# Attention with a score bias on one Trainium2 core: rearranging the first ten microseconds of a kernel bound by ScalarE

## The chip, the cores and the metric

The kernel runs on one core of a Trainium2 chip. The metric is the device time of one execution in microseconds (us); lower is better. The *span* is the stretch from the first to the last instruction in the profile of an execution; it was 1.7 to 3.0 us shorter than the time. Engines: PE (TensorE matmul; PEld is its weight load), DVE (VectorE), ACT (ScalarE), POOL (GpSimd), SP (SyncE).

## The reference

Shapes are 4 x 8 x 1024 x 64 for q, k and v, and 1 x 1 x 1024 x 1024 for the bias, all float32.

```python
scores = scale * np.matmul(q, k.transpose(0, 1, 3, 2)) + bias
scores_max = np.max(scores, axis=-1, keepdims=True)
attn = np.exp(scores - scores_max) / (np.sum(np.exp(scores - scores_max), axis=-1, keepdims=True) + 1e-8)
return np.matmul(attn, v).astype(np.float32)
```

## The kernel before

The kernel uses exp(s + b) = exp(s) * exp(b). PE makes scores in PSUM, "slots" of up to three banks of 128 x 512; ACT takes exp of a slot (tile `E`); DVE multiplies it by exp(bias) (tile `eb`); PE multiplies the result with V, in which a column of ones gives the row sum. exp(bias) is made once, in four pieces: PE transposes the bias (tile `pb`), ACT takes its exp. All loads but the first four go through one software DMA queue issued by POOL, in the order below.

```python
nc.sync.dma_start(out=k0f[:, :, :2]..., in_=kf[0]...)      # first k quarter, float32
nc.scalar.dma_start(out=q0f[0]..., in_=qf[0]...)           # q, head 0, first half
nc.sync.dma_start(out=q0f[1]..., in_=qf[0]...)             # q, head 1, first half
nc.sync.dma_start(out=k0f[:, :, 2:]..., in_=kf[0]...)      # second k quarter
# ... POOL: k half, q half, first bias half, k and q of pair 1
wm = ps_s.tile([P, 3, HQ], F32, tag="s", name="wm")
for i in range(6):                                         # dummy matmuls: keep PE busy
    nc.tensor.matmul(wm[:, i % 3, :], zeros[:, :P], zeros[:], start=True, stop=True)
# ...
nc.vector.tensor_copy(qr0[:, 0, :QC, :], q0f[0][:])        # casts to bf16
nc.scalar.copy(kr0[:, :, :2, :], k0f[:, :, :2, :])
nc.scalar.copy(qr0[:, 1, :QC, :], q0f[1][:])
pq0 = q_trans(0, ...); pk0 = k_trans(0, 2, "xb"); q_out(0, pq0)
nc.scalar.copy(kr0[:, :, 2:QC, :], k0f[:, :, 2:, :])       # the late k cast
nc.scalar.copy(kT0[:, :2, :], pk0[:])                      # the first k copy
pq1 = q_trans(1, ...)
s_fill(0); q_out(1, pq1); s_exp(0)
pk1 = k_trans(2, 2, "xa")
s_fill(1); nc.vector.tensor_copy(kT0[:, 2:QC, :], pk1[:]); s_exp(1)
# from here on a small scheduler in Python orders the rest; order is ACT's order:
order = [("S", g) for g in range(2, NS)]
for at, x in ((5, (0, 0)), (7, (0, 4)), (11, (1, 0)), (13, (1, 4))):
    order.insert(at, ("B",) + x)                           # the four bias exps
# ... behind the second k half's copy:
nc.vector.memset(vall[:, :, :, D:D1], 1.0)                 # ones
load_v(0); nc.gpsimd.dma_start(out=btraw[:, QC:, :], ...)  # V of pair 0, second bias half
load_v(1); load_qk(2)
```

The scheduler's result is a fixed order of instructions on each engine; each engine carries it out in that order.

The softmax here doesn't subtract the row's maximum and nothing guards it: scores larger than these inputs give would overflow.

Of the kernel before, what the change touches and what calls it, by code (L numbers as in the profile page):

```python
# [15 lines left out]
def kernel(  # L16
# [15 lines left out]
    nc = tc.nc  # L32
    B, H, S, D = q.shape
    P = 128
    NCH = S // P
    D1 = D + 1
    NP = B * H // 2
    scale = 1.0 / (D ** 0.5)
    HQ = S // 2
    QC = NCH // 2  # L40
# [5 lines left out]
    bf_ = bias.rearrange("a b (p c) k -> p (a b c) k", p=P)  # L46
# [12 lines left out]
    btraw = consts.tile([P, NCH, S], BF)  # L59
# [3 lines left out]
    vall = consts.tile([P, 2 * NP, NCH, D1], BF)  # L63

    k0f = consts.tile([P, 2, QC, D], F32)
    q0f = [consts.tile([P, QC, D], F32, name=f"q0f{t}") for t in range(2)]
    zeros = consts.tile([P, HQ], BF)
# [4 lines left out]
    def load_qk(pr):  # L72
        qr = raw.tile([P, 2, NCH, D], BF, name="qr")
        kr = raw.tile([P, 2, NCH, D], BF, name="kr")
        nc.gpsimd.dma_start(out=kr.rearrange("p t c d -> p t (c d)"), in_=kf[pr])  # L75
        nc.gpsimd.dma_start(out=qr.rearrange("p t c d -> p t (c d)"), in_=qf[pr])  # L76
        raws[pr] = (qr, kr)

    def load_v(pr):
        for t in range(2):  # L80
            nc.gpsimd.dma_start(out=vall[:, 2 * pr + t, :, :D], in_=vf[pr, :, t])  # L81
# [30 lines left out]
    NS = len(slots)  # L112
# [3 lines left out]
    def e_at(b, n):  # L116
        if b // ET not in etiles:
            etiles[b // ET] = ep.tile([P, ET, HQ], BF, name="E")
        return etiles[b // ET][:, b % ET:b % ET + n, :]
# [3 lines left out]
    def s_fill(g):  # L123
        ps = ps_s.tile([P, 3, HQ], F32, tag="s", name="ps")
        open_ps[("S", g)] = ps
        for j, b in enumerate(slots[g]):
            pr, h, qh, kc = banks[b]
            qT, kT = trs[(pr, 0)], trs[(pr, 1)]
            nc.tensor.matmul(ps[:, j, :], kT[:, kc, :], qT[:, h, qh * HQ:(qh + 1) * HQ],  # L129
                             start=True, stop=b not in late_bias)  # L130
            if b in late_bias:
                nc.tensor.matmul(ps[:, j, :], ident[:], braw[:, late_bias[b], :], start=False, stop=True)

    def s_exp(g):
        n = len(slots[g])
        nc.scalar.activation(e_at(slots[g][0], n), open_ps.pop(("S", g))[:, :n, :], ACTF.Exp, scale=scale)  # L136
# [26 lines left out]
    def late_bias_pe(tag):  # L163

        px = ps_x.tile([P, 2, HQ], BF, tag=tag, name="px")
        for j in range(2):
            for i in range(QC):
                nc.tensor.transpose(px[:, j, i * P:(i + 1) * P],
                                    btraw[:, QC + i, :].rearrange("p (kp kc) -> p kc kp", kc=NCH)[:, NCH - 2 + j, :],
                                    ident[:])  # L170

        def copy():
            nc.vector.tensor_scalar(braw[:], px[:], 1.0 / scale, None, op0=ALU.mult)
        return copy
# [39 lines left out]
    with tc.manual_schedule():  # L214
# [9 lines left out]
        qr0 = raw.tile([P, 2, NCH, D], BF, name="qr")  # L224
        kr0 = raw.tile([P, 2, NCH, D], BF, name="kr")
        raws[0] = (qr0, kr0)
        kT0 = kvp.tile([P, NCH, P], BF, name="kT")
# [11 lines left out]
        load_qk(1)  # L239

        wm = ps_s.tile([P, 3, HQ], F32, tag="s", name="wm")
        for i in range(6):
            nc.tensor.matmul(wm[:, i % 3, :], zeros[:, :P], zeros[:], start=True, stop=True)

        def k_trans(c0, n, tag):
            px = ps_x.tile([P, n, P], BF, tag=tag, name="px")
            for c in range(n):
                for t in range(2):
                    nc.tensor.transpose(px[t * D:(t + 1) * D, c, :], kr0[:, t, c0 + c, :], ident[:])
            return px  # L250

        def q_trans(t, px):
            for c in range(QC):
                nc.tensor.transpose(px[t * D:(t + 1) * D, c, :], qr0[:, t, c, :], ident[:])
            return px

        def q_out(t, px):
            nc.vector.tensor_copy(qT0[t * D:(t + 1) * D, t, :HQ],
                                  px[t * D:(t + 1) * D, :, :].rearrange("p c q -> p (c q)"))

        nc.vector.tensor_copy(qr0[:, 0, :QC, :], q0f[0][:])
        nc.scalar.copy(kr0[:, :, :2, :], k0f[:, :, :2, :])
        nc.scalar.copy(qr0[:, 1, :QC, :], q0f[1][:])
        pq0 = q_trans(0, ps_x.tile([P, QC, P], BF, tag="xa", name="px"))
        pk0 = k_trans(0, 2, "xb")
        q_out(0, pq0)
        nc.scalar.copy(kr0[:, :, 2:QC, :], k0f[:, :, 2:, :])
        nc.scalar.copy(kT0[:, :2, :], pk0[:])
        pq1 = q_trans(1, ps_s.tile([P, 3, 2 * HQ], BF, tag="s", name="pq").rearrange(
            "p b (c q) -> p (b c) q", q=P)[:, :QC, :])  # L270
        s_fill(0)
        q_out(1, pq1)
        s_exp(0)
        pk1 = k_trans(2, 2, "xa")
        s_fill(1)
        nc.vector.tensor_copy(kT0[:, 2:QC, :], pk1[:])
        s_exp(1)



        COLD = 4600
        EXP, EXP0, QK, AV, TP = 427, 45, 216, 170, 350
        MUL, COPYQ, COPYK, EVAC, SEM = 600, 650, 420, 620, 80
        order = [("S", g) for g in range(2, NS)]
        for at, x in ((5, (0, 0)), (7, (0, 4)), (11, (1, 0)), (13, (1, 4))):
            order.insert(at, ("B",) + x)
        NO = len(order)
        T0 = 5250.0
        t_act, t_pe, t_dve = T0 + 1620, T0 + 550, T0 + 600
        filled = []  # L290
        act_end = []
        x_free = {"xa": T0 + 600, "xb": T0}
        x_unit = {}
        bias_at = [13000, 22000]
        raw_at = {0: (5900, 6600), 1: (15500, 16500), 2: (26000, 28500)}
        pieces = [(0, 1, 1), (0, 0, 1)]
        for pr in range(1, NP):
            pieces += [(pr, 1, 0), (pr, 0, 0), (pr, 1, 1), (pr, 0, 1)]

        pieces.append((NP, 0, 0))  # L300
        raw_at[NP] = (T0, T0)
        piece_end = {(0, 1, 0): T0 + 600, (0, 0, 0): T0}
        eb_at = {}
        exp_at = {0: T0 + 600, 1: T0 + 1620, 2: T0 + 1620}
        mul_at = {}
        mul_next = 0
        av_order = []
# [7 lines left out]
        def unit_of(b):  # L315
            return banks[b][:3]
# [10 lines left out]
        def act_end_of(i):  # L327
            if i < 0:
                return T0
            if i < len(act_end):  # L330
# [30 lines left out]
        def pe_piece():  # L361
            if not pieces:
                return None
            pr, which, half = pieces[0]
            if pr not in raw_at or (pr < NP and pr not in raws):
                return None
            i = min(len(filled), NO - 1)
            while order[i][0] != "S":
                i -= 1
            at = slots[order[i][1]][0]  # L370
            if at < (pr - 2) * 32 + 8:
                return None

            left = NCH - av_next % NCH
            busy = x_unit.get(unit_of(av_order[av_next])) if av_next % NCH else None
            tags = sorted((x_free[x], x) for x in x_free if x != busy)
            if busy and left < 4 and at < pr * 32 - 16:
                return None
            if not busy and av_next and at < pr * 32 - 16 and tags[0][0] + SEM < t_pe and len(tags) > 1 and tags[1][0] > t_pe:
                return None  # L380
            free, tag = tags[0]
            ready = max(free + SEM, raw_at[pr][1 - which])

            def emit(t):
                pieces.pop(0)
                copy = transpose_pe(pr, which, half, tag) if pr < NP else late_bias_pe(tag)
                cost = COPYK if which else COPYQ
                x_free[tag] = 1e12

                def run(t2):  # L390
                    copy()
                    if (pr, which, half) == (0, 1, 1):
                        nc.vector.memset(vall[:, :, :, D:D1], 1.0)  # L393
                        load_v(0)
                        nc.gpsimd.dma_start(out=btraw[:, QC:, :], in_=bf_[:, QC:, :])
                        load_v(1)
                        load_qk(2)
                    x_free[tag] = t2 + cost
                    piece_end[(pr, which, half)] = t2 + cost
                    if pr < NP and which == 0 and half == 1:  # L400
                        if pr + 3 < NP:
                            load_qk(pr + 3)
                            raw_at[pr + 3] = (t2 + 7000, t2 + 7000)
                        if pr + 2 < NP:
                            load_v(pr + 2)
                dve_q.append((t + pe_cost(t, TP) + SEM, 0, cost, run))
            return ready, TP, emit
# [84 lines left out]
        while len(act_end) < NO or av_next < NB or dve_q:  # L492
# [12 lines left out]
            if who == 0:  # L505
                i = a[2]
                item = order[i]
                t_act = t + a[1]
# [11 lines left out]
            elif who == 1:  # L520
                if d in dve_q:
                    dve_q.remove(d)
                t_dve = t + d[2]
                d[3](t)
            else:
                t_pe = t + pe_cost(t, p[1])
# [31 lines left out]
```

## Time and profile before

| | before |
|---|---|
| time, median of the first three executions | 251.33 us (251.31 to 251.9) |
| span of the profiled execution | 250.1 us |
| ACT busy | 239.9 us (96%) |
| exp 3 (the exp of slot 3) starts | 10.92 us |
| second bias half lands | 24.2 us |
| third bias exp starts | 25.56 us, after 0.24 us of idle |

The lines are shown in the prediction. In a timeline line the first number is the start in us, the second the time from the first start to the last end of the merged instructions, then engine, source line, operation and tiles; brackets hold the idle time of the engine before it and what ended it.

### The profile page before, as it was taken

The page shows a single profiled execution, that of the slowest core. Times are in us where ns is not written, and L with a number is a line of the kernel's source. Part 1 is how long each engine was busy: PE and PEld are TensorE (multiplying, and loading weights), DVE is VectorE, ACT ScalarE, POOL GpSimd, SP SyncE. Part 2 cuts the span into 40 slices and gives each one's busy share as a digit, 9 for nine tenths or more (in the row PEclk, how much of TensorE's full clock was granted, in tenths as well). Part 3 has the DMA queues.
Part 4 walks back from the last instruction along what each step waited for, and adds up shares of the span by engine and source line. Part 5 has one row for each costly group of instructions (what it writes and reads, how often), then busy time and mean ns, then how long its engine had stood idle before and what let it go on. Part 6 is the DMA issues. An engine that isn't in the chain of part 4 may idle for free.

```text
span 250.1 us, 7172 instructions
## 1 busy us (share of the span) xinstructions
PE 231.5 (93%) x3152; PEld 141.8 (57%) x3152; DVE 219.1 (88%) x375; ACT 239.9 (96%) x182; POOL 53.7 (21%) x74
## 2 busy tenths in 40 slices
PE   6868999999999999999999999999999999999893
PEld 2345756556566556665566656666665555665552
DVE  4209699999999999999999999999999999998884
ACT  4799999999999999999999999999999999999991
POOL 8183505161040131302213055016000000000000
PEclk9999999999999999999999999999999999999999
DMA  6999997799186393920935859728911102020112
GB/s 119 189 187 181 192 144 122 55 155 180 45 134 79 82 89 99 114 87 8 167 62 103 91 74 184 83 84 105 111 44 42 46 0 88 3 84 3 62 46 64
DMA packets 48175, 23.79 MB, mean 95 GB/s; under 512 B 34448, under 2 KB 44048, under 8 KB 47888
## 3 DMA queue, kind: packets, MB, share of 16 engines
q0 software_dynamic: 42272, 14.42, 53.4%
q1 hardware_dynamic: 5584, 8.72, 9.6%
q8 instruction: 24, 0.39, 0.6%
q10 hardware_dynamic: 288, 0.20, 0.3%
q14 instruction: 7, 0.06, 0.1%
HBM read 29.36 MB, written 8.39 MB: 151 GB/s over the span
## 4 chain that ended last, share of the span: by engine, by line
ACT 75%; PE 16%; DVE 5%; DMA 1%; issue 1%; SPq 0%; DVEq 0%; ACTq 0%
ACT E L136 73%; PE ps L129 11%; PE px L89 2%; ACT eb L149 2%; PE po L186 2%; DVE E L161 2%; DMA k0f<-in_k_dram 1%; DVE E L158 1%; PE pb L144 1%; DVE qT L98 1%; DVE E L155 1%; DVE oall L206 0%; DVE rs L196 0%; SPq L218 0%; SPq L216 0%
## 5 line engine op out<-in xcount | busy, mean ns | idle before, releaser
L136 ACT ACTIVATE E<-ps 128x1536 bf16<-128x1536 f32 (+2 forms) x172 | 230.2, 1709 | 2.2 <-PE ps L129 2.2
L129 PE MATMUL ps<-qT,kT 128*128 128x512 bf16 x512 | 139.5, 381 | 10.0 <-ACT E L136 5.4
L186 PEld LDWEIGHTS <-E 128*128 128x128 bf16 x2048 | 83.1, 98 | 38.8 <-DVE E L158 2.1
L158 DVE TENSOR_TENSOR E<-E,eb 128x2048 bf16<-128x2048 bf16 x82 | 98.9, 1217 | 1.3 <-ACT E L136 0.7
L186 PE MATMUL po<-vall,E 128*128 128x65 bf16 x2048 | 92.9, 194 | 1.8 <-DVE E L158 0.8
L129 PEld LDWEIGHTS <-kT 128*128 128x128 bf16 x512 | 45.5, 97 | 44.7 <-issue 9.4
L161 DVE TENSOR_TENSOR E<-E,eb 128x1024 bf16<-128x1024 bf16 x84 | 55.8, 684 | 7.7 <-ACT eb L149 6.8
L81 POOL DMA_DIRECT2D vall<-in_v_dram x32 | 28.2, 885 | 10.0 <-DVE vall L393 5.5
L75 POOL DMA_DIRECT2D kr<-in_k_dram x15 | 10.6, 704 | 91.8 <-PE px L89 91.5
L206 DVE TENSOR_TENSOR oall<-po,rs 128x256 f32<-128x256 f32 x63 | 26.7, 425 | 2.2
L98 DVE TENSOR_TENSOR qT<-px,mask 128x1024 bf16<-128x1024 bf16 x31 | 21.5, 694 | 3.3 <-PE px L89 2.0
L102 DVE COPY kT<-px 128x512 bf16<-128x512 bf16 x31 | 13.1, 422 | 4.9 <-PE px L89 4.4
L76 POOL DMA_DIRECT2D qr<-in_q_dram x15 | 10.8, 720 | 18.5 <-PE px L89 16.8
L196 DVE RECIPROCAL rs<-po 128x4 f32<-128x4 f32 x64 | 11.4, 178 | 3.8 <-PE po L186 3.3
L89 PE MATMUL px<-ident,kr 128*64 128x128 bf16 x248 | 13.0, 227 | 0.2 <-DVE oall L206 0.2
L89 PE MATMUL px<-ident,qr 128*64 128x128 bf16 x248 | 13.1, 228 | 0.0
L89 PEld LDWEIGHTS <-qr 128*64 128x64 bf16 x248 | 8.1, 111 | 7.9 <-issue 6.4
L89 PEld LDWEIGHTS <-kr 128*64 128x64 bf16 x248 | 8.1, 110 | 7.1 <-issue 5.4
L149 ACT ACTIVATE eb<-pb 128x2048 bf16<-128x2048 bf16 x4 | 7.5, 1877 | 0.2 <-PE pb L144 0.2
L144 PE MATMUL pb<-ident,btraw 128*128 128x128 bf16 x64 | 4.6, 225 | 1.5 <-ACT eb L149 1.0
L144 PEld LDWEIGHTS <-btraw 128*128 128x128 bf16 x64 | 4.5, 147 | 1.9 <-issue 1.7
L155 DVE TENSOR_TENSOR E<-E,eb 128x1024 bf16<-128x1024 bf16 (+1 forms) x6 | 4.6, 776 | 0.6 <-ACT E L136 0.6
(39 smaller groups left out, 22.0 us busy)
## 6 DMA issues: line engine op xcount, KB each, us to landing
out_dram<-oall SPq DMA_DIRECT2D x30, 256.0 KB, 2.1
vall<-in_v_dram POOLq DMA_DIRECT2D x32, 128.0 KB, 6.5
kr<-in_k_dram POOLq DMA_DIRECT2D x15, 256.0 KB, 4.2
qr<-in_q_dram POOLq DMA_DIRECT2D x15, 256.0 KB, 5.7
btraw<-in_bias_dram POOLq DMA_DIRECT2D x2, 1024.0 KB, 10.0
out_dram<-oall SPq DMA_DIRECT2D x3, 128.0 KB, 1.7
k0f<-in_k_dram SPq DMA_DIRECT2D x2, 128.0 KB, 3.0
q0f<-in_q_dram ACTq DMA_DIRECT2D x1, 128.0 KB, 2.6
```

The costliest lines, as they stand in the source:

```text
L81: nc.gpsimd.dma_start(out=vall[:, 2 * pr + t, :, :D], in_=vf[pr, :, t])
L89: nc.tensor.transpose(px[t * D:(t + 1) * D, c, :], src[:, t, half * QC + c, :], ident[:])
L98: nc.vector.tensor_tensor(dst[:, :, half * HQ:(half + 1) * HQ], px.rearrange("p c q -> p (c q)").unsqueeze(1).to_broadcast([P, 2, HQ]), ma ...
L102: nc.vector.tensor_copy(dst[:, half * QC:(half + 1) * QC, :], px[:])
L129: nc.tensor.matmul(ps[:, j, :], kT[:, kc, :], qT[:, h, qh * HQ:(qh + 1) * HQ], start=True, stop=b not in late_bias)
L136: nc.scalar.activation(e_at(slots[g][0], n), open_ps.pop(("S", g))[:, :n, :], ACTF.Exp, scale=scale)
L144: nc.tensor.transpose(ps[:, j, i * P:(i + 1) * P], btraw[:, qh * QC + i, :].rearrange("p (kp kc) -> p kc kp", kc=NCH)[:, k0 + j, :], ident[:])
L149: nc.scalar.activation(eb[:, qh, k0:k0 + 4, :], open_ps.pop(("B", qh, k0))[:, :4, :], ACTF.Exp)
L158: nc.vector.tensor_tensor(e, e, eb[:, qh, kc:kc + 2, :].unsqueeze(2).to_broadcast([P, 2, 2, HQ]), op=ALU.mult)
L161: nc.vector.tensor_tensor(e, e, eb[:, qh, kc:kc + 1, :].to_broadcast([P, n, HQ]), op=ALU.mult)
L186: nc.tensor.matmul(acc[:, i, :], e[:, 0, i * P:(i + 1) * P], vall[:, 2 * pr + h, kc, :], start=(kc == 0 and i == 0), stop=(kc == NCH - 1), ...
L206: nc.vector.tensor_tensor(oall[:, c0:c0 + QC, :], acc[:, :, :D], rs[:].to_broadcast([P, QC, D]), op=ALU.mult)
```

## The change

The intent is an earlier and gapless start of ACT's stream of exps. The second q cast leaves ACT for DVE, the late k cast goes behind the copy that frees the first score matmul, and the second k half is transposed before slot 2, so that slot 3 does not wait for it. The ones, and with them the V loads, come sooner. The dummy matmuls are trimmed to end before the first data come.

```diff
-        for i in range(6):
-            nc.tensor.matmul(wm[:, i % 3, :], zeros[:, :P], zeros[:], start=True, stop=True)
+        def dummy(n):
+            nc.tensor.matmul(wm[:, 0, :n], zeros[:, :P], zeros[:, :n], start=True, stop=True)
+        for i in range(5):
+            dummy(HQ)
+        dummy(P)
 ...
-        nc.scalar.copy(qr0[:, 1, :QC, :], q0f[1][:])
+        nc.vector.tensor_copy(qr0[:, 1, :QC, :], q0f[1][:])
 ...
-        nc.scalar.copy(kr0[:, :, 2:QC, :], k0f[:, :, 2:, :])
         nc.scalar.copy(kT0[:, :2, :], pk0[:])
         pq1 = q_trans(1, ...)
-        s_fill(0)
         q_out(1, pq1)
+        nc.scalar.copy(kr0[:, :, 2:QC, :], k0f[:, :, 2:, :])
+        dummy(P)
+        s_fill(0)
         s_exp(0)
         pk1 = k_trans(2, 2, "xa")
         s_fill(1)
         nc.vector.tensor_copy(kT0[:, 2:QC, :], pk1[:])
+        nc.vector.memset(vall[:, :, :, D:D1], 1.0)
         s_exp(1)
+        pk2 = k_trans(QC, QC, "xb")
+        s_fill(2)
+        nc.vector.tensor_copy(kT0[:, QC:, :], pk2[:])
+        s_exp(2)
+        load_v(0)
+        nc.gpsimd.dma_start(out=btraw[:, QC:, :], in_=bf_[:, QC:, :])
+        load_v(1)
+        load_qk(2)
 ... (the scheduler's starting times are set to match; the issues leave their old place)
```

ACT's order is unchanged from slot 3 on. On PE the second q half's transposes, which stood ahead of slot 3, now stand behind slot 4.

More of the change, by code (lines that the diff above doesn't have):

```diff
@@ L270 @@
             "p b (c q) -> p (b c) q", q=P)[:, :QC, :])
+        q_out(1, pq1)
+        nc.scalar.copy(kr0[:, :, 2:QC, :], k0f[:, :, 2:, :])
+        dummy(P)
         s_fill(0)
-        q_out(1, pq1)
         s_exp(0)
@@ L283 @@
         MUL, COPYQ, COPYK, EVAC, SEM = 600, 650, 420, 620, 80
-        order = [("S", g) for g in range(2, NS)]
-        for at, x in ((5, (0, 0)), (7, (0, 4)), (11, (1, 0)), (13, (1, 4))):
+        order = [("S", g) for g in range(3, NS)]
+        for at, x in ((4, (0, 0)), (6, (0, 4)), (10, (1, 0)), (12, (1, 4))):
             order.insert(at, ("B",) + x)
         NO = len(order)
-        T0 = 5250.0
-        t_act, t_pe, t_dve = T0 + 1620, T0 + 550, T0 + 600
+        T0 = 7000.0
+        t_act, t_pe, t_dve = T0 + 1400, T0, T0 + 300
         filled = []
         act_end = []
-        x_free = {"xa": T0 + 600, "xb": T0}
+        x_free = {"xa": T0 - 500, "xb": T0 + 200}
         x_unit = {}
-        bias_at = [13000, 22000]
-        raw_at = {0: (5900, 6600), 1: (15500, 16500), 2: (26000, 28500)}
-        pieces = [(0, 1, 1), (0, 0, 1)]
+        bias_at = [13000, 21500]
+        raw_at = {0: (5900, 7000), 1: (15500, 16500), 2: (26000, 28500)}
+        pieces = [(0, 0, 1)]
         for pr in range(1, NP):
@@ L301 @@
         raw_at[NP] = (T0, T0)
-        piece_end = {(0, 1, 0): T0 + 600, (0, 0, 0): T0}
+        piece_end = {(0, 1, 0): T0, (0, 0, 0): T0, (0, 1, 1): T0 + 200}
         eb_at = {}
-        exp_at = {0: T0 + 600, 1: T0 + 1620, 2: T0 + 1620}
+        exp_at = {x: T0 + (0 if x < 3 else 1400) for x in range(6)}
         mul_at = {}
@@ L391, in run @@
                     copy()
-                    if (pr, which, half) == (0, 1, 1):
-                        nc.vector.memset(vall[:, :, :, D:D1], 1.0)
-                        load_v(0)
-                        nc.gpsimd.dma_start(out=btraw[:, QC:, :], in_=bf_[:, QC:, :])
-                        load_v(1)
-                        load_qk(2)
                     x_free[tag] = t2 + cost
```

## The prediction

> **What bounds the kernel now.** I began with the page's busy shares: ScalarE (ACT) is busy 239.9 us of a span of 250.1 us, so it idles 10.2 us in all, and its own work outside the prologue is not touched by the change. VectorE has 219.1 us and PE 231.5 us. The chain of work that ended last says the same:
>
> ```profile
> PE 231.5 (93%) x3152; PEld 141.8 (57%) x3152; DVE 219.1 (88%) x375; ACT 239.9 (96%) x182; POOL 53.7 (21%) x74
> ...
> ACT 75%; PE 16%; DVE 5%; DMA 1%; issue 1%; SPq 0%; DVEq 0%; ACTq 0%
> ```
>
> So the change can only pay through ACT's idle time. The timeline of ACT over the first 30 us (start, duration, what, and in brackets the idle time before it and what ended it) shows where that is:
>
> ```profile
> 3.58 0.41 ACT L262 CAST kr<-k0f 128x256 bf16<-128x256 f32 x1 [0.89 <-DMA k0f<-in_k_dram]
> 3.92 0.41 ACT L263 CAST qr<-q0f 128x256 bf16<-128x256 f32 x1
> 5.00 0.40 ACT L267 CAST kr<-k0f 128x256 bf16<-128x256 f32 x1 [0.68 <-DMA k0f<-in_k_dram]
> 5.31 0.37 ACT L268 COPY kT<-px 128x256 bf16<-128x256 bf16 x1
> 6.37 0.60 ACT L136 ACTIVATE E<-ps 128x512 bf16<-128x512 f32 x1 [0.70 <-PE ps L129]
> 7.69 1.02 ACT L136 ACTIVATE E<-ps 128x1024 bf16<-128x1024 f32 x1 [0.72 <-PE ps L129]
> 8.97 1.45 ACT L136 ACTIVATE E<-ps 128x1536 bf16<-128x1536 f32 x1 [0.26 <-PE ps L129]
> 10.92 5.48 ACT L136 ACTIVATE E<-ps 128x1536 bf16<-128x1536 f32 x4 [0.49 <-PE ps L129]
> ...
> 21.19 4.13 ACT L136 ACTIVATE E<-ps 128x1536 bf16<-128x1536 f32 x3
> 25.56 1.88 ACT L149 ACTIVATE eb<-pb 128x2048 bf16<-128x2048 bf16 x1 [0.24 <-PE pb L144]
> ```
>
> The reader is to see two things. First, ACT has waits of 0.68, 0.70, 0.72, 0.26 and 0.49 us before the fourth exp (I call the exps of the score slots exp 0, 1, 2, 3); from 10.92 us on it runs without a gap, up to the third bias exp (eb) at 25.56 us, which waits 0.24 us for the bias transposes. After that no ACT idle of over 0.1 us follows until the tail. Second, the change works on the first stretch alone, and eb at 25.56 is a second gate behind it. What feeds that gate is in the timeline of PE and POOL at that time:
>
> ```profile
> 24.10 0.42 PE L186 MATMUL po<-vall,E 128*128 128x65 bf16 x8 [0.37 <-DVE E L158]
> 24.33 1.06 PEld L144 LDWEIGHTS <-btraw 128*128 128x128 bf16 x16
> 24.36 1.17 PE L144 MATMUL pb<-ident,btraw 128*128 128x128 bf16 x16
> 24.50 0.88 POOL L81 DMA_DIRECT2D vall<-in_v_dram  x1 [3.80 <-DMA btraw<-in_bias_dram]
> ```
>
> The second half of the bias is issued at 13.19 us (L395), and the tile's view gives 11.0 us as its longest time to landing: 24.2 us. POOL, which waits for that landing too, goes on at 24.50. PE starts the transposes at 24.36, so at most about 0.15 us after the data. In the table by stretch the DMA share stays full all along:
>
> ```profile
> 8.00:12.00 4.00, 3.53 (x25) 1.49 (x24) 1.32 (x3) 3.25 (x3) 0.57 (x1) 1.00 1.03 211
> 12.00:16.00 4.00, 2.51 (x21) 1.51 (x21) 0.00 (x0) 4.00 (x4) 4.00 (x6) 1.00 1.52 174
> 16.00:20.00 4.00, 3.19 (x49) 2.33 (x47) 1.79 (x4) 4.00 (x4) 2.56 (x5) 1.00 1.20 195
> 20.00:24.00 4.00, 3.20 (x33) 1.53 (x31) 3.70 (x6) 4.00 (x4) 0.70 (x1) 1.00 1.50 174
> ```
>
> The last two columns are the DMA share and GB/s: the software queue is never without work from about 4 us to 35 us.
>
> **What the Trainium skill says.** (1) "TensorE: Matmul & The Clock Gate", section "What's actually happening": PE starts at half rate, and a free-running window of about 3.4 us that was busy enough releases it. The trace agrees: the weight loads of the first score matmuls start at 7.02, 7.45 and 7.88 us, 0.43 us apart, while three such matmuls at 12.42 us take 0.81 us together, which is 0.22 us apart. So PE was still slow while it fed exps 1 and 2; the clock column says 1.00 throughout and does not show this. (2) "DMA: Bandwidth & Descriptors", section "Queues, rings and completion order": each engine consumes its ring's descriptors in order (said of the hardware queues). The software queue's landings agree: they come in the order of issue. (3) The same page, "Latency and other measured facts", says that two of the DMA engines are usually slower, with contention from the software descriptor rings as a guess. The trace is compatible: V of pair 0 needed until 18.5 us although the q load ahead of it landed at 15.7, and later V loads land about 1 us apart. (4) "ScalarE: Activation LUTs", "What ACT_TABLE_LOAD costs": back-to-back ACTIVATEs overlap by about 93 ns. Here four exps of 1.45 us take 5.48 us, 1.34 us each, so it agrees.
>
> **The change part by part.** All times below are from the start of the span; "est." is worked out from the rows above.
> - *Dummies.* Six of 0.427 us become five and one of 128 columns (0.107 us): they end 0.32 us sooner, near 3.5 us, so the first q transposes start after VectorE's cast (3.32 + 0.29 = 3.61) at 3.65 est. and not 3.91.
> - *Second q cast to VectorE.* It removes 0.41 us from ACT and adds about 0.29 us to an idle VectorE; its data lands near 3.9 us either way, so its transposes hardly move.
> - *Late k cast behind the first k copy.* Before, the copy stood behind a cast that waited until 5.00 for its DMA, and ran at 5.31. Now it can run when the k transposes end, 4.6 to 4.75 est., and ends near 5.0. The first score matmul goes from 5.73 to about 5.0 to 5.1, and exp 0 from 6.37 to about 5.7. The late cast then runs at 5.0 to 5.4, as before, so the next k transposes come at 5.45 est. in place of 6.27, and exp 1 near 6.9 in place of 7.69.
> - *Second k half ahead of slot 2.* Eight transposes come before the three matmuls of slot 2. Before, slot 2 followed slot 1 at once, and then came 16 transposes, a copy of 0.42 us and the wait for it. Now: transposes from 6.8 (8.87 less the 2.1 us of five matmuls, carried to the new slot 1), slot 2 at about 7.35 and ready at 7.35 + 2 x 0.427 + 0.63 = 8.83 if PE is still slow. Exp 2 then runs 8.85 to 10.2, and slot 3 is ready long before, so exp 3 starts at 10.2 in place of 10.92: 0.7 us gained. If PE comes to full rate near 6.9 (fewer gaps on PE make a busy window likelier), slot 2 is ready at 7.9 and exp 3 starts at about 9.3: 1.6 us gained.
> - *Ones ahead of the V loads.* The memset (0.27 us) moves from 10.85 to about 6.3, so POOL issues V and the second bias half 4 to 5 us sooner. In a queue that is busy all along and kept in order, that by itself brings no byte earlier.
> - *Order behind the prologue.* ACT's order is unchanged from exp 3 on. On PE the third bias transposes now stand ahead of the eight AV matmuls that waited for VectorE at 24.10. That makes them wait for the landing alone.
>
> So ACT reaches the gate 0.7 to 1.6 us sooner. Beside that gate its idle time was 0.24 us. If the bias half lands at 24.2 as before, the transposes run 24.25 to 25.4, eb starts at 25.45, and all that is kept is about 0.1 us; the idle time before eb becomes 0.24 + 0.7 to 1.6 less 0.1. Every microsecond that the landing itself moves forward is kept, up to the head start. So gain = 0.1 + (24.2 - new landing), at most about 1.7.
>
> **The rivals.** *A, the landing does not move* (about 40%): for it, the full DMA share and the ordered queue. Time 251.33 - 0.1 = 251.2. *B, it moves by 0.3 to 1.5 us* (about 50%): the excess of some 1.7 us in V of pair 0 falls in the time in which POOL writes descriptors without a pause (its busy time is 4.00 of 4 us at 12 to 16); with these issues moved to 6.5 to 10 us, that stall may shrink. The author's own table also sets the arrival of the second bias half 0.5 us earlier. Time 251.33 - 0.1 - 0.3 to 1.5: 249.8 to 250.9, its middle 250.4. *C, it gets worse* (about 10%): the first bias half (issued at 3.97, needed by PE at about 13.5 now and not 15.11) is slowed by POOL's earlier descriptor work, or the k half lands too late for its new place. Time 251.4 to 251.9.
>
> **Range and chances.** 0.4 x 251.2 + 0.5 x 250.4 + 0.1 x 251.6 = 250.8. The range is 250.0 to 251.5; it takes in the spread of the kernel before (251.31 to 251.9) on the side of A. Two per cent is 5.0 us, and ACT's whole idle time ahead of eb is less than that if the start-up before 3.58 us is left out, so same has 0.98, and the other two 0.01 each.
>
> **What would show it right or wrong.** In the changed profile: the first score matmul at 5.0 to 5.2; exp 0 near 5.7; exp 1 near 6.9; exp 3 between 9.2 and 10.3; score matmuls 0.43 or 0.22 us apart at 7.3 say which end. Then the idle time before the third eb: about 1 us or more with "PE pb" as the releaser shows A; near zero with bias transposes well before 24 us shows B. I am wrong if exp 3 starts after 10.5 (the prologue chain is not what I think), or if the time falls by more than 1.7 us, or if a new ACT wait turns up at 12 to 24 us.

## The result, and the profile after

The changed kernel takes 251.29 us (median of 6, 250.83 to 251.81), the kernel before 251.25 us (median of 6, 250.47 to 251.9). The ratio is 1.0007 with a 95% interval of 0.9985 to 1.0029: the same. By their record, which calls a difference under 2% the same, every run that has a verdict is the same as the kernel before; what is said below of smaller differences rests on the intervals and on the spans.

The profiled execution has a span of 249.1 us, 1.0 us less than the first profile of before. ACT's timeline in it:

```profile
4.54 0.37 ACT L272 COPY kT<-px 128x256 bf16<-128x256 bf16 x1 [0.53 <-PE px L254]
4.95 0.41 ACT L276 CAST kr<-k0f 128x256 bf16<-128x256 f32 x1
5.65 0.60 ACT L136 ACTIVATE E<-ps 128x512 bf16<-128x512 f32 x1 [0.30 <-PE ps L129]
6.42 7.92 ACT L136 ACTIVATE E<-ps 128x1024 bf16<-128x1024 f32 x6 [0.17 <-PE ps L129]
...
24.54 1.88 ACT L149 ACTIVATE eb<-pb 128x2048 bf16<-128x2048 bf16 x1 [1.21 <-PE pb L144]
```

The exps run from 6.42 us without a gap; exp 3 starts at 8.87 us (taken from the single records of the merged line), 2.05 us sooner than in the first profile of before. But the idle time ahead of the third bias exp has grown from 0.24 to 1.21 us. The timeline of PE and POOL there:

```profile
23.32 1.04 PEld L144 LDWEIGHTS <-btraw 128*128 128x128 bf16 x16 [1.69 <-DMA btraw<-in_bias_dram]
23.33 1.18 PE L144 MATMUL pb<-ident,btraw 128*128 128x128 bf16 x16 [1.57 <-ACT E L136]
23.57 0.88 POOL L81 DMA_DIRECT2D vall<-in_v_dram  x1 [4.48 <-DMA btraw<-in_bias_dram]
```

PE's weight load waited 1.69 us for the bias to land (23.28 us), and ACT waited for PE. That is half of the story. The other half is the durations of the first score matmuls, in the tile view of `ps` (durations in ns as min/median/max, then first and last start). The first profile of before, 4 to 10.2 us:

```profile
L129 PE MATMUL ps<-qT,kT x7: 587/634/634, 5.7 to 9.9; 128*128 128x512 bf16 x7
```

The changed kernel, 4 to 8 us:

```profile
L129 PE MATMUL ps<-qT,kT x9: 376/379/390, 5.2 to 7.9; 128*128 128x512 bf16 x9
```

In the first, PE was at half rate up to slot 3; in the second it was at full rate for all of them. The trace's clock record gives the moment: 10.30 us in the first profile of before, 5.25 us in this one. The experiments ask whether that belongs to the kernel or to the single execution.

### The profile page after: what moved, and what is told of

It is laid out like the page before. It is cut to its first block, busy times and chain, and to the rows that moved or that the text cites. A ratio compares the mean times of both kernels' runs of the same rounds, so it can differ in the third digit from the quotient of the medians.

```text
span 249.1 us, 7119 instructions
## 1 busy us (share of the span) xinstructions
PE 226.9 (91%) x3098; PEld 141.4 (57%) x3153; DVE 219.2 (88%) x376; ACT 239.6 (96%) x181; POOL 53.6 (22%) x74
## 4 chain that ended last, share of the span: by engine, by line
ACT 79%; PE 14%; DVE 4%; issue 1%; DVEq 0%; ACTq 0%
ACT E L136 76%; PE ps L129 8%; ACT eb L149 3%; PE po L186 2%; PE px L89 2%; PE wm L244 1%; DVE E L161 1%; DVE E L158 1%; DVE E L155 1%; DVE qT L98 1%; PE pb L144 0%; PE px L254 0%; DVE kT L102 0%; PE px L259 0%; DVE oall L206 0%
## 5 line engine op out<-in xcount | busy, mean ns | idle before, releaser
L129 PE MATMUL ps<-qT,kT 128*128 128x512 bf16 x457 | 134.6, 377 | 11.9 <-ACT E L136 5.2
L75 POOL DMA_DIRECT2D kr<-in_k_dram x15 | 10.5, 701 | 94.7 <-PE px L89 91.8
L102 DVE COPY kT<-px 128x512 bf16<-128x512 bf16 x30 | 12.6, 421 | 2.4 <-PE px L89 1.9
L76 POOL DMA_DIRECT2D qr<-in_q_dram x15 | 10.8, 717 | 18.3 <-PE px L89 16.8
L89 PE MATMUL px<-ident,kr 128*64 128x128 bf16 x240 | 12.4, 225 | 0.3 <-DVE oall L206 0.3
## 6 DMA issues: line engine op xcount, KB each, us to landing
btraw<-in_bias_dram POOLq DMA_DIRECT2D x2, 1024.0 KB, 11.5
```

What stands on the lines that cost most here:

```text
L89: nc.tensor.transpose(px[t * D:(t + 1) * D, c, :], src[:, t, half * QC + c, :], ident[:])
L102: nc.vector.tensor_copy(dst[:, half * QC:(half + 1) * QC, :], px[:])
L129: nc.tensor.matmul(ps[:, j, :], kT[:, kc, :], qT[:, h, qh * HQ:(qh + 1) * HQ], start=True, stop=b not in late_bias)
```

## The experiments

Theory one, *the gate*: the third bias exp cannot start before the second bias half lands plus about 1.25 us, so a head start ahead of it is lost. Theory two, formed after e5, *the clock*: the head start depends on when PE comes to full rate, which the change makes late more often. "Slow" and "late" mean this half rate at the start. The rival throughout is that the rest of the kernel, or one part of the change, holds the time.

The table collects all 14 profiles. "Full rate" is from the trace's clock record. In that record the clock drops again 238.93 us after its release in nine profiles and 242.35 us after it in five: a difference of 3.41 us, the length of the stretches used here. "Busy share" is PE's busy share in the 3.41 us before that moment and, after the stroke, in the 3.41 us before those (a dash where that stretch starts more than 1 us before PE's first work). I worked it out from the matmuls' starts, a matmul of 512 columns counted as 0.427 us, of 384 as 0.320 and of 128 as 0.107 us (their spacing in the traces while slow), and time in which two overlap counted once. "Waits" are ACT's idle times of 0.1 us or more behind exp 3.

| profile | full rate, us | busy share | exp 3, us | waits, us | span, us |
|---|---|---|---|---|---|
| before | 10.30 | 0.92 / 0.61 | 10.92 | 0.24 | 250.07 |
| e1, before again | 5.58 | 0.78 / - | 9.93 | 0.34 | 249.16 |
| e4 | 9.66 | 0.91 / 0.66 | 10.66 | 0.22 | 249.77 |
| e6 | 9.22 | 0.89 / 0.73 | 10.43 | 0 | 249.22 |
| e11 | 4.06 | 0.74 / - | 9.47 | 0 | 248.24 |
| changed | 5.25 | 0.82 / - | 8.87 | 1.21 | 249.06 |
| e2, changed again | 5.14 | 0.84 / - | 9.46 | 0.53 + 0.26 | 249.27 |
| e3 | 7.80 | 0.74 / 0.71 | 10.08 | 0.33 | 249.31 |
| e5 | 9.44 | 0.85 / 0.64 | 10.96 | 0 | 249.76 |
| e7 | 10.88 | 0.83 / 0.72 | 10.74 | 0 | 249.52 |
| e8 | 10.70 | 0.87 / 0.68 | 10.74 | 0.27 | 249.90 |
| e9 | 5.68 | 0.83 / - | 9.24 | 0.86 | 248.98 |
| e10 | 9.60 | 0.88 / 0.74 | 10.74 | 0 | 249.52 |
| e12 | 10.59 | 0.92 / 0.73 | 10.79 | 0 | 249.61 |

In every row the span less exp 3 less the waits is 238.8 to 239.0 us. So nothing behind exp 3 makes a difference but those waits, and the whole question is exp 3 and the waits. The time less the span differs by up to 1.3 us between executions, so the spans are the finer measure.

### e1 and e2: both kernels once more

No edit. Expected of e1:

> The kernel before, once more, for the spread of its start. First theory (the second bias half is the gate): the third bias exp starts 1.2 to 1.4 us after that half lands, or when the exps ahead of it end, whichever is later, and nothing ahead of it counts. In the first profile of before PE went to full rate near 10.3 us and the half landed at 24.2 us; if both are matters of the single execution, they differ here (landing anywhere from 23.2 to 24.3 us), and the time follows the landing. Rival (the later landing is a property of the kernel before, made by its late V issue): it lands at 24.2 us again, within 0.2 us, with V of pair 0 again landing near 18.5 us.

Expected of e2:

> The changed kernel once more. Gate theory: the bias half lands at 23.2 to 24.2 us and the third bias exp starts 1.2 to 1.3 us later, with about 1.0 to 2.0 us of ACT idle ahead of it, whatever exp 3 did. Rival (the head start is lost elsewhere): no idle time before that exp in this execution, and a wait of 1 us or more at some later place.

Measured: 251.2 us for before, 251.03 us for the changed kernel, one execution each. The timeline of ACT, kernel before (e1):

```profile
9.93 5.48 ACT L136 ACTIVATE E<-ps 128x1536 bf16<-128x1536 f32 x4 [0.73 <-PE ps L129]
...
24.66 1.88 ACT L149 ACTIVATE eb<-pb 128x2048 bf16<-128x2048 bf16 x1 [0.34 <-PE pb L144]
```

and the changed kernel (e2):

```profile
8.11 6.82 ACT L136 ACTIVATE E<-ps 128x1536 bf16<-128x1536 f32 x5 [0.68 <-PE ps L129]
15.47 1.88 ACT L149 ACTIVATE eb<-pb 128x2048 bf16<-128x2048 bf16 x1 [0.53 <-PE pb L144]
...
24.75 1.88 ACT L149 ACTIVATE eb<-pb 128x2048 bf16<-128x2048 bf16 x1 [0.26 <-PE pb L144]
```

The kernel before now had full rate at 5.58 us and its bias half landed at 23.4 us, with V of pair 0 at 17.2 and not 18.5 us. So the 1 us between the two first spans was a matter of the executions, not of the change. The rival of e1 falls. In e2 the bias half landed at 23.5 us and the third bias exp started at 24.75 us, so the gate holds, though not with the 1 to 2 us of idle that I had named: the head start had already gone. The k half landed at 6.9 us (5.85 in the first profile of the changed kernel), too late for its new place ahead of slot 2, so exp 2 waited 0.68 us. The first bias half landed at 14.2 us (13.0 there), so the first bias exp waited 0.53 us. The gate has sisters.

### e3 and e4: the second bias half one place ahead in the queue

```diff
-        load_v(0)
+        load_v(0, (0,))
         nc.gpsimd.dma_start(out=btraw[:, QC:, :], in_=bf_[:, QC:, :])
+        load_v(0, (1,))
         load_v(1)
```

e3 is this in the changed kernel, e4 in the kernel before (`load_v` gets a second argument: which of the two heads).

> The changed kernel with one queue entry moved: the second bias half is issued after the first V load and not after the second, so it should land about 0.95 us sooner (near 22.3 us). Gate theory: ACT's idle time before the third bias exp falls from 1.21 us to about 0.3 us and the time falls by 0.7 to 1.0 us against the kernel before (ratio near 0.9965). Rival (the gain is lost elsewhere, the wait before that exp is only where it shows): the time stays within 0.2 us of the kernel before, and the idle time turns up at a later place.

> The same move of the queue entry in the kernel before, without the change of the prologue. Gate theory: there ACT comes to the third bias exp only 0.24 us too early, so no more than about 0.25 us is won (ratio 0.999 to 1.0), however early the half lands; its prologue becomes the bound. Rival (the order of the loads alone makes the time): it wins as much as the changed kernel does with the same move, 0.7 us or more.

Measured: e3 251.37 us, ratio 1.0008 (0.9981 to 1.0034); e4 251.26 us, ratio 0.9996 (0.9969 to 1.0024). The expectation for e3 failed at its first step: the half landed at 23.5 us in both, no sooner than behind two V loads. The trace's packet records show the last data packet of that half ending at 21.50 us in e3 and 21.47 us in e4, so 2 us passed between data and landing; in the changed kernel it was 22.67 us and 23.28 us. A landing is counted by 16 increments of a semaphore: 15 of them had come by 21.77 us in e3 and 21.79 us in e4, and the last came at 23.52 and 23.55 us. Why is left open. And e3 reached full rate only at 7.80 us, so exp 3 started at 10.08 us. The two results do not tell the theories apart.

### e5 and e6: the third and fourth bias exps one slot later

```diff
-        for at, x in ((4, (0, 0)), (6, (0, 4)), (10, (1, 0)), (12, (1, 4))):
+        for at, x in ((4, (0, 0)), (6, (0, 4)), (11, (1, 0)), (13, (1, 4))):
```

e6 is the same in the kernel before (11 to 12, 13 to 14).

> The changed kernel with the third and fourth bias exps one score slot later in the schedule, so ACT has one more exp of 1.34 us to do before it comes to the gate. In five of six traces so far the span is the start of the third bias exp plus 224.5 us. Gate theory: the idle time ahead of that exp goes (under 0.2 us), the head start shows at last, the span is the start of exp 3 plus 238.9 us (247.8 to 249.0 us for exp 3 at 8.9 to 10.1) and the time falls by 0.7 to 1.5 us against the kernel before (ratio 0.994 to 0.997). Rival (the rest of the kernel is bound by VectorE or AV work, not by ACT's start): the time stays within 0.3 us of before, with new ACT waits behind 30 us, since the multiplications of the second half now start later.

> The same move of the two bias exps in the kernel before. Gate theory: ACT came to the gate only 0.24 to 0.34 us too early there, so 0.2 to 0.4 us is won and no more (ratio near 0.999); exp 3 at about 10 to 11 us is then the bound. Rival (the order of the exps is itself what helps): as much is won as in the changed kernel.

Measured: e5 251.45 us, ratio 1.0007 (0.9979 to 1.0035); e6 250.4 us, ratio 0.9966 (0.993 to 1.0002). e6 won 0.34%, more than the 0.2 to 0.4 us that I expected, but its interval takes in 1. Neither profile has a wait at the gate. That is no test of the gate, though: in e5 the half landed at 22.37 us, and the exp at its old place, 1.34 us earlier at about 25.3 us, would not have waited either (in e6 it would have met the gate just on time). And e5 won nothing. ACT's timeline of e5:

```profile
6.34 0.60 ACT L136 ACTIVATE E<-ps 128x512 bf16<-128x512 f32 x1 [0.52 <-PE ps L129]
7.66 1.02 ACT L136 ACTIVATE E<-ps 128x1024 bf16<-128x1024 f32 x1 [0.72 <-PE ps L129]
9.62 6.82 ACT L136 ACTIVATE E<-ps 128x1536 bf16<-128x1536 f32 x5 [0.93 <-PE ps L129]
...
26.61 1.88 ACT L149 ACTIVATE eb<-pb 128x2048 bf16<-128x2048 bf16 x1
```

and the tile view of `ps` in it, 4 to 9.3 us:

```profile
L129 PE MATMUL ps<-qT,kT x6: 582/619/634, 5.7 to 8.9; 128*128 128x512 bf16 x6
```

PE was slow up to 9.44 us, exp 2 waited 0.93 us for the eight transposes and three slow matmuls now ahead of it, and exp 3 started at 10.96 us, no sooner than in the kernel before. So the gate alone does not explain the result: in this execution there was no head start to lose. Five of the six spans of e5 stand at 249.5 to 249.8 us, one at 248.9. The changed kernel's six are alike: 249.1 once, 249.5 to 249.7 five times. The kernel before spreads wider in the same rounds as e5: 248.5 to 249.1 us seven times and 249.6 to 250.4 four times. That made the second theory. What PE did between the dummies and the first transposes of e5:

```profile
2.49 1.17 PE L244 MATMUL wm<-zeros 128*128 128x512 bf16 x3
4.26 0.53 PE L259 MATMUL px<-ident,qr 128*64 128x128 bf16 x3 [0.60 <-DVE qr L266]
```

The first q load landed at 3.88 us there (3.27 in the first profile of the changed kernel). The trimmed dummies were used up at 3.45 us, and PE had a hole of 0.8 us up to 4.26 us (the bracket says 0.60, since it counts from the end of the last dummy's latency, not of its columns) in the stretch that should have released its clock: busy share 0.64.

A late load was not the whole of it. Where the first q load landed at 3.51 to 3.65 us (e3, e6, e7, e8, e10, e11, e12), VectorE's cast behind it took 0.42 to 0.56 us and not 0.29, and ended at 4.09 to 4.10 us in all seven. DVE's timeline of e7:

```profile
3.53 0.56 DVE L266 CAST qr<-q0f 128x256 bf16<-128x256 f32 x1 [0.64 <-DMA q0f<-in_q_dram]
```

POOL was busy with the issue of the q half from 3.25 to 3.98 us in each of them; whether that held up the cast was not tested.

### e7 and e8: both moves, and the late V loads back

e7 has the edits of e3 and e5 together. e8 is e5 with the ones, V loads and second bias half issued behind the copy of the second q half.

> Both moves in the changed kernel: bias half issued after the first V load, and its exp one slot later. The first move brought the landing no sooner in e3 and e4 (23.5 us), so gate theory: the same as e5 within 0.3 us, without idle time ahead of the third bias exp. Rival (the landing still binds): e7 is faster than e5 by 0.5 us or more.

> e5 with one part of the change undone: ones, V loads and the second bias half issued behind the q half as late as before (near 11 us in place of 7.6 to 8.2 us). If the early issue does nothing, because the queue is full and ordered: landings as in e5 (bias half 23.2 to 24.2 us), time as e5 within 0.3 us. Rival (the late issue costs landing time, as the first trace of before seemed to show with V of pair 0 at 18.5 us): V of pair 0 lands 1 us or more later than in e5 and the bias half at 24 us or later.

Measured: e7 251.05 us, ratio 0.999 (0.996 to 1.002), half landed at 22.1 us, no wait at the gate, exp 3 at 10.74 us with full rate at 10.88 us. Its time is 0.4 us below e5's, between what was expected and what the rival said. With the half landed that early, the exp would not have waited at its old place either, so this too is no test of the gate. The six spans are 248.2 to 249.7 us, three of them at 249.5 or more. e8: 250.85 us, ratio 0.9987 (0.995 to 1.0024). Its V loads were issued at 14.2 us, later than I had meant, since the q half is now copied later, and its four spans are 248.7 to 249.9 us; the bias half landed at 25.5 us and the moved exp waited again:

```profile
26.75 1.88 ACT L149 ACTIVATE eb<-pb 128x2048 bf16<-128x2048 bf16 x1 [0.27 <-PE pb L144]
```

So an issue that late (16.0 us for the bias half itself) is late enough to hurt the landing, in one look. Issued at 11.5 to 13.2 us, as in the kernel before, the half landed at 23.1 to 24.2 us in five profiles (before, e1, e4, e6, e11); issued at 9.1 to 10.2 us it landed at 22.1 to 24.5 us in the other eight. The spread of the executions is larger than any effect of the earlier issue.

### e9 to e12: PE kept busy

All four have the bias exps of e5 and e6. e9 is e5 with more dummy work:

```diff
-        for i in range(5):
+        for i in range(6):
             dummy(HQ)
         dummy(P)
 ...
-        dummy(P)
+        dummy(3 * P)
         s_fill(0)
```

e10 is e5 with six full dummies and nothing else. e11 is e6, the kernel before, with six dummies of 128 columns ahead of the first score matmul:

```diff
+        for i in range(6):
+            nc.tensor.matmul(wm[:, 0, :P], zeros[:, :P], zeros[:, :P], start=True, stop=True)
         s_fill(0)
         q_out(1, pq1)
```

e12 is e9 with `pk2` transposed behind `s_fill(2)`.

> e5 with more dummy matmuls: six of 512 columns and one of 128 at the start (they end near 3.9 us in place of 3.45), and one of 384 columns in place of 128 ahead of the first score matmul. Clock theory (the head start exists only where PE comes to full rate early; whether it does is decided by whether a 3.41 us stretch of PE, at a phase that differs by execution, is filled to about 74% or more; the shorter dummies left holes): PE at full rate by 8.1 us at the latest in the profile, exp 3 at 8.9 to 9.9 us, most of the spans at 247.9 to 248.9 us and the time 0.6 to 1.3 us below the kernel before (ratio 0.995 to 0.9975). Rival (the second k half ahead of slot 2 and the gate alone explain it): spans stay near 249.5 us as in e5.

> e5 with only the cut of the dummies undone: six of 512 columns as in the kernel before. Clock theory: more executions come to full rate early than in e5 (where five of six spans stood at 249.5 us or more) but not all; the spans fall in two groups, near 248.2 and near 249.5 us, and the time is 0.3 to 0.8 us below e5. Rival (0.32 us of dummies are no matter): spans as in e5, five of six at 249.5 us or more.

> e6 (the kernel before, bias exps one slot later) with six dummies of 128 columns ahead of the first score matmul, where PE stood idle from 4.8 to 5.7 us. Clock theory: full rate by 8.1 us, exp 3 near 9.6 to 9.9 us (it was 9.93 with full rate at 5.6 us, 10.4 to 10.9 without), spans mostly 248.3 to 248.8 us, with less spread than e6 (248.0 to 249.5). Rival: spans as in e6.

> e9 with one part of the change undone: the second k half transposed behind slot 2, as before, with the rest of the change and the fuller dummies kept. If that part is what saves the wait ahead of exp 3 once PE is fast: that wait comes back as 0.3 to 0.7 us and the time is 0.3 to 0.7 us above e9. Rival (the part is neutral, since it puts its transposes on the path to exp 2 instead): within 0.2 us of e9, exp 2 earlier and exp 3 at the same time.

| | time, us | ratio (95%) | spans of the six executions, us |
|---|---|---|---|
| before, same rounds | 251.24 | 1 | 248.5 to 250.0; 3 of 11 at 249.0 or less |
| e9 | 250.38 | 0.9966 (0.994 to 0.9992) | 248.4, 248.5, 248.5, 248.6, 248.9, 249.0 |
| e10 | 250.12 | 0.9968 (0.9939 to 0.9997) | 248.1, 248.2, 248.3, 248.4, 249.5, 249.5 |
| e11 | 250.11 | 0.9956 (0.9933 to 0.9978) | 248.1, 248.1, 248.2, 248.2, 248.2, 248.2 |
| e12 | 250.0 | 0.9962 (0.9932 to 0.9992) | 247.7, 248.0, 248.0, 248.3, 249.4, 249.6 |

The clock theory holds. e10 undoes nothing but the cut of the dummies and shows the two groups as expected, four spans at 248.1 to 248.4 us and two at 249.5 us (by time it is 1.3 us below e5, more than expected). e9 and e11 have no slow group at all. As e5 to e8 ran in other rounds and on another chip than e9 to e12, and with few executions each, the counts are better pooled: with the trimmed dummies and the bias exps moved (e5, e7, e8) nine of 16 spans stand at 249.4 us or more, with the fuller dummies (e9, e10, e12) four of 18.

The busy shares agree. Every stretch that released the clock has 0.742 or more, every one ahead of it 0.739 or less. The transposes have to be counted as work for that: without them, stretches that released it go down to 0.40 and others go up to 0.65. With 0.74 as the line and every phase of the stretches equally likely, I estimate from the slow-starting traces how often full rate comes by 7 us: in 52% to 56% of phases for the kernel before (before, e4, e6), 21% to 22% for the changed start-up (e3, e5, e7, e8; at least 34% to 38% with the early loads of its two other profiles), 66% for e10 and 80% for e12, whose start-up is that of e9.

In e11 the kernel before, without any of the change's rearrangement, gets its score matmuls at full rate from the first one (tile view of `ps`, 4 to 9.3 us) and ACT's exps early:

```profile
L129 PE MATMUL ps<-qT,kT x10: 376/379/390, 5.6 to 9.3; 128*128 128x512 bf16 x10
```

```profile
6.80 2.37 ACT L136 ACTIVATE E<-ps 128x1024 bf16<-128x1024 f32 x2 [0.17 <-PE ps L129]
9.47 5.48 ACT L136 ACTIVATE E<-ps 128x1536 bf16<-128x1536 f32 x4 [0.29 <-PE ps L129]
```

All four beat the kernel before, and e11 has the lowest ratio, 0.44% below it, with the smallest spread of all: small, but clear of the noise. As the changed kernel is the same as the kernel before within 0.3%, e11 beats both. But part of each gain can be the moved bias exps: e6, which has them alone, stands at 0.9966, and its interval overlaps e11's. What the dummies add shows in the spans, 248.1 to 248.2 us in e11 against 248.0 to 249.5 us in e6. In e9 ACT is still earlier, and meets the first bias half, which landed at 14.3 us:

```profile
6.79 7.92 ACT L136 ACTIVATE E<-ps 128x1024 bf16<-128x1024 f32 x6 [0.17 <-PE ps L129]
15.57 1.88 ACT L149 ACTIVATE eb<-pb 128x2048 bf16<-128x2048 bf16 x1 [0.86 <-PE pb L144]
```

That fits e9's spans, which stand above e11's, but I have one profile of it only. The profiles of e9 and e11 do test the gate. The second bias half landed at 23.88 us in e9 and at 23.06 us in e11, and the moved exp did not wait (ACT's timeline, the first line of e9, the second of e11):

```profile
25.83 1.88 ACT L149 ACTIVATE eb<-pb 128x2048 bf16<-128x2048 bf16 x1
25.08 1.89 ACT L149 ACTIVATE eb<-pb 128x2048 bf16<-128x2048 bf16 x1
```

At its old place, 1.34 us earlier, it would have come some 0.6 us ahead of the gate in both (an estimate, with the gate 1.25 us behind the landing).

e12 does not support the view that the second k half ahead of slot 2 is what pays: without it the time is 250.0 us against 250.38 us, and its fastest span, 247.7 us, is the lowest. Its profile fell in an execution in which full rate came late, so where exp 2 and exp 3 stand in the others is not shown. By the ratios (0.9962 against 0.9966) these runs show no effect of the part.

## Why the prediction was right or wrong

The time, 251.29 us, lies in the range and in "same", and it is rival A's time (251.2) almost to the tenth. The centre of 250.8 us was 0.5 us too low. The agreement with A is in part luck: A's account fits the execution that was profiled, but in others of the changed kernel there was probably no head start to lose. By its steps:

- **ACT's idle time as the bound, and eb as a second gate: right.** All 14 spans follow exp 3 and the waits behind it. In the changed kernel's profile 1.21 us of idle stand before the third bias exp with PE `pb` as the releaser, which is what I had named as the sign of A. Where that wait would have stood again, moving the exp by a slot took it away (e9, e11).
- **"Any microsecond that the landing moves forward is kept", with half the weight on a landing moved by the early V issue (rival B): this term was mis-sized, and it made the centre wrong.** The landing of 24.2 us that I took for the kernel's was the latest of five profiles without the changed start-up (23.1 to 24.2 us). In the first profile of the changed kernel the half landed at 23.28 us, 0.93 us sooner, just as B said; in e1 it landed at 23.38 us without the change. The excess of 1.7 us in V of pair 0 was there in the first profile and not in e1. So I read a property of the kernel out of one execution.
- **"If PE is still slow, exp 3 starts at 10.2, 0.7 us gained": wrong.** With PE slow, exp 3 started at 10.74 to 10.96 us in e5, e7, e8 and e10, against 10.43 to 10.92 us for the kernel before and its variants (before, e4, e6), and past the 10.5 us that I had named as a sign of being wrong. The gain there is nil. Two terms were missing. The first loads landed later in these executions (first q load at 3.5 to 3.9 us, not 3.3) and in three of them the cast behind it took 0.42 to 0.56 us, not 0.29, so exp 0 came at 6.12 to 6.34 and not 5.7 us. That is most of the miss. And exp 1 needs the same 1.3 us behind exp 0 as before, so slot 2, now behind eight transposes, was ready at 9.4 to 9.6 and not 8.83 us.
- **"Fewer gaps on PE make a busy window likelier": wrong, and backwards.** I counted the trim of the dummies as 0.32 us saved. In fact it opened a hole behind them whenever the first load came late. The changed kernel had full rate at 5.1 to 5.3 us in both its profiles, but five of its six spans are those of the slow group (249.5 to 249.7 us; 238.9 us and exp 3 at 10.6 to 10.8 us). None of those five was profiled, and the span alone does not prove it: e2, early, has 249.27 us with its waits at the bias halves. The mean clock helps for two of the five. It leaves out the slow start but counts the drop at the end, and 0.999 puts the drop at 248.8 to 249.3 us; 70 or 71 stretches of 3.413 us before that, as in all 14 profiles, lie 9.8 to 10.3 us and 6.4 to 6.9 us, and a stretch that ends at the latter is too empty in the four slow-starting profiles (share of at most 0.62). So these two were very likely late; the other three stay open. With the dummies back (e10) the slow group shrank, and with the holes filled (e9, e11) it was gone.
- **The full-rate case, exp 3 at about 9.3 us: right, but not all of it a gain.** Exp 3 came at 8.87 us in the first profile and 9.46 us in e2. The 1.6 us set this against a kernel before at half rate; at the same clock (e1) that had 9.93 us, so the gain is 0.5 to 1.06 us. What of it is left at the end is what the two bias halves let through.
- **Single times.** The first score matmul came at 5.24 us (5.0 to 5.2 expected), though its k copy ended at 4.91 us. The extra dummy before it ran from 4.85 to 5.14 us; in the trace PE's wait ahead of slot 0 is for its own semaphore too, which it is not in the kernel before. That fits a wait for that dummy, since both write the same PSUM buffer. I had counted that dummy as free. Exp 0 at 5.65 us is as predicted, exp 1 at 6.42 us earlier than the 6.9 us of the slow case.
- **Rival C**, the k half or the first bias half too late for its new need, was given 10%. Both turned up: in e2 (0.68 and 0.53 us), the second in e9 (0.86 us).

So the expected gain went two ways. When PE's clock comes up early, the head start is real, and most of it is lost again in waits for the bias. When it comes up late, which the shorter dummies very likely made more frequent, there is no head start.

## What to carry to other kernels

Before a start-up is rearranged, profile it more than once: from one execution to the next the first q load landed at 3.3 to 3.9 us here and PE's full rate came at 4.1 to 10.9 us, and two single profiles showed a gain of 1.0 us that did not exist. Here PE's holes during the start-up mattered more than the chain of casts and copies: with the holes filled and the bias exps moved, the kernel with the shorter chain (e9) was no faster than the one without (e11). Warm-up work trimmed to the earliest arrival of the data can cost the clock when the data are late. When a chain is shortened ahead of a transfer, look up when the next transfer lands, and give the waiting engine other work there first.

## What the Trainium skill lacked or had wrong

- "TensorE: Matmul & The Clock Gate" says that a busy window of about 3.4 us releases the clock, and that the window runs free. Both agree with the traces (full rate at 4.06 to 10.88 us in 14 profiles; the clock drops again 238.93 us after its release in the first profile, which is 70 times 3.413 us). It does not say how busy is busy enough: here every stretch with a share of 0.742 or more released it and none of 0.739 or less did, so the line is near 0.74, as far as my count of busy time goes. The page's remark that the ramp costs under 1% of a typical kernel agrees in size (spans of e10: 248.1 to 248.4 against 249.5 us, 0.5%), but here it was larger than the change itself.
- "DMA: Bandwidth & Descriptors" gives a fixed cost of about 2 us, mostly the receipt of the write, and its table calls it about constant. For the second bias half the time from the end of its last data packet to its landing was 0.3 us (before), 0.6 us (changed) and 2.0 us (e3), on the same queue. What makes the difference these runs do not show; in e3 one of the 16 increments alone was 1.75 us behind the others.
- No page that I used says that the clock column of the profile stands at 1.00 while PE is still at half rate; the matmul durations of 634 and 379 ns show it.
